# Two Strassen pairs of the recurrence's projections placed ahead of attention, and a planner that counts eight transfers under way

## The chip, the cores and the metric

One core of one Trainium2 chip runs the whole layer in one launch. The metric is the device time in microseconds of one execution; the figure for a kernel is the median of several runs. The engines are TensorE (PE, with its weight loads PEld), VectorE (DVE), ScalarE (ACT), GpSimd (POOL) and the queue of SyncE (SP), which issues nearly all transfers.

## The reference

One layer over 1024 frames of width 1024, float32. The parts that matter here:

```python
proj = x @ w_in
q_a, k_a, v_a, f_a, q_b, f_b, i_b, g_b, gate_a, gate_b = jnp.split(proj, IN_SPLITS, axis=-1)
y_a = fox_attention(q_a, k_a, v_a, log_sigmoid(f_a + b_f))      # 8 heads of 64, causal softmax
# the recurrence: 4 heads of 128
f  = lbh + (1.0 - lbh) * jax.nn.sigmoid(f_b)                    # forget gates
qh = jax.nn.silu(q_b)                                           # queries
o_b = hgrn2_chunkwise(qh, 1.0 - f, i_b, jnp.log(f))
y_b = rms_norm(o_b) * norm_g * jax.nn.sigmoid(g_b)
merged = sigmoid(gate_a) * (y_a @ w_pa) + sigmoid(gate_b) * (y_b @ w_pb)
x = layer_norm(ALPHA * x + merged @ w_o, ...)
x = layer_norm(ALPHA * x + swiglu_ffn(x, w_ff_in, w_ff_out), ...)
```

## The kernel before

Each float32 product is made of three matmuls on a high and a low part (`mm3`: high by high, high by low, low by high). The parts come from `split`, which is one ACT cast and one DVE subtraction. A matmul of full size has a stationary tile of 128x128 and 512 moving columns.

The stages in order are: the values by Strassen's method (to about 85 us); queries and keys of attention, four pairs of heads by Strassen's method (`qk_strassen`, called by `qk_all` in the order of the table `QORDER`); attention, eight heads (`attention`); the recurrence, four heads (`hgrn`); the gates by Strassen's method; the merge and output projection; the first layer norm; the feed-forward block; the second layer norm. Strassen's method takes the two halves of the contraction and the two halves of the frames, and makes two output blocks with 7 products of 12 matmuls, 84 in all. The plain way takes 2 x 48 = 96.

The recurrence needs three projections for each of its heads: the forget gate (index 1 of `w_b`), the query (index 0) and the output gate (index 2). `hgrn_project` makes each the plain way: `weights` loads and splits 512 KB, `project` runs 24 matmuls for each half of the frames into a bank named `bps`, ACT applies the sigmoid, and DVE multiplies for the query. That is 12 projections and 576 matmuls. They depend on nothing in attention, so they stand between attention's own matmuls and between those of the recurrence, as do parts of the gates (`gate_part`, banks named `ge`).

No engine's order is written by hand. Every call is recorded by `Plan`, and `schedule` places the calls on the engines one by one by modelled costs (`cost`), latencies (`LAT`), free buffers (each tile has a tag, and each tag a number of buffers) and due times found by `latest`. `improve` repeats that 36 times and keeps the best plan. So a change in one place reorders the whole program. For transfers the planner has one stream with a rate, a start latency, and a wait per issue on SP. `plan.behind` makes a call wait for another one.

Names that the steps use: `qk_d` is the DRAM buffer through which queries and keys pass; `q2_0`, `k2_0`, `kl_0` are the query, high key and low key of attention head 0 as loaded from it; `box1` holds the forget sums and the causal mask; `kb` is a tag with 4 buffers, `hl` one with 2. The keys `k2` and `kl` take `kb`. Two `kb` buffers also hold the operand of product p3 until the last pair of queries and keys is through. `wb` is a weight of the recurrence, `lp`, `dg`, `kdt`, `up`, `op`, `ot` are the recurrence's banks, and `hk`, `qf`, `at` its working tiles.

Of the kernel before, what the change touches and what calls it, by code (L numbers as in the profile page):

```python
# [16 lines left out]
P = 128  # L17
S = 1024
# [15 lines left out]
FIRST = 8  # L34
WARM = 7
ROUNDS = 36
QORDER = ((0, "hl", ("s", "pt", "s")), (1, "kb", ("h", "pv", "h")), (2, "hl", ("s", "pt", "s")), (3, "hl", ("h", "s", "h")))
MARGIN = 1.06
SLACK = 400.0
SWITCH = 300.0  # L40
# [23 lines left out]
class Plan:  # L64

    LAT = {"PE": 197.0, "ACT": 131.0, "DVE": 128.0, "POOL": 66.0, "SP": 2500.0}
    OWN = {"PE": 0.0, "ACT": 0.0, "DVE": 127.0, "POOL": 60.0, "SP": 2500.0}
    SOFT, LANDS, RATE = 950.0, 1050.0, 190.0  # L70
    SETS = {AF.Exp: 0, AF.Ln: 0, AF.Sigmoid: 1, AF.Silu: 2}

# [69 lines left out]
    def cost(self, eng, method, outs, ins, kw):  # L142
        o = outs[0]
        n = o.free_size()
        psum = any(str(a.space).endswith("PSUM") for a in ins)
        if eng == "PE":
            dt = ins[0].dtype
            if method == "transpose":
                return 109.0
            if dt == F32:  # L150
                return 2 * max(112.0, n / 1.2 + 2)
            return n / 2.4 + 13.4 if n > 128 else 111.0
        if eng == "ACT":
            d = n / 1.2 + (52 if psum else 94) + 95 * (o.partition_size() == DH)
            if "accum_out" in kw:
                d += 93
            return d + 93 * sum(isinstance(kw.get(x), bass.AP) for x in ("scale", "bias"))
        if eng == "DVE":
            scal = sum(1 for a in ins if a.free_size() == 1 and n > 1)
            two = method in ("tensor_scalar", "tensor_copy") and not psum  # L160
            if method == "reciprocal":
                return 90.0
            if method == "tensor_tensor_scan":
                return n * 2.1 + 69
            if method == "copy_predicated":
# [12 lines left out]
        return float(o.nbytes()) / 300.0  # L178

    def kind(self, call):  # L180
        return next((self.SETS.get(x) for x in call[2] if isinstance(x, AF)), None)
# [1 line left out]
    def schedule(self, slack, wait):  # L183
# [12 lines left out]
        free = {q: 600.0 for q in self.queues}  # L196
        dma_free = 0.0
        ring = [0.0] * RING
        fifo, slots = {}, {}
        for name, i in sorted(self.first.items(), key=lambda kv: (self.turn[kv[1]], kv[1])):  # L200
            tag, bufs = self.tiles[name][:2]
# [13 lines left out]
        while done < len(calls):  # L215
            best = None
            for q, av in avail.items():
                for i in av:
                    t = max(free[q], ready[i])
                    ok = True  # L220
                    need = {}
                    for name in calls[i][6]:
                        if name in held:
                            continue
                        tag = self.tiles[name][0]
                        k = need.get(tag, 0)
                        if tag not in LOOSE and name not in self.loose and (len(fifo[tag]) <= k or fifo[tag][-1 - k] != name):
                            ok = False
                            break
                        if len(slots[tag]) <= k:  # L230
                            ok = False
                            break
                        t = max(t, sorted(slots[tag])[k][0] + 60)
                        need[tag] = k + 1
                    if not ok:
                        continue
                    if self.lands[i]:
                        t = max(t, ring[-RING])
                    if q == "ACT":
                        kind = self.kind(calls[i])  # L240
                        if kind is not None and kind != table:
                            t += wait
                    if best is None or (t, self.rank[i]) < best[:2]:
                        best = (t, self.rank[i], i, q)
# [9 lines left out]
            if q == "SP":  # L254
                start = max(t + 100, dma_free)
                dma_free = start + d
                free[q] = t + 500
                fin = dma_free
            else:
                if q == "ACT":  # L260
                    kind = self.kind(c)
                    if kind is not None and kind != table:
                        table = kind
                        t -= wait
                        d += 1283
# [125 lines left out]
def trunk(ctx: ExitStack, tc, a: dict, out: bass.AP):  # L391
# [341 lines left out]
    def qk_strassen(p, wtags, btags, last=False):  # L733

        g, u = (take(t, [KC, P], f"w{n}{p}_r") for t, n in zip(wtags, "qk"))
        for b, t in enumerate((g, u)):
            sync.dma_start(t, a["w_qk"][b, p])
        b11, b12, b21, b22 = g[:, :4], u[:, :4], g[:, 4:], u[:, 4:]
        p1, p5 = (half("ph", f"qk{p}_{i}") for i in ("p1", "p5"))
        oa, ob, oc = (bank(t, f"qk{p}_{t}") for t in btags)  # L740

        def mul(n, src, o, first):
            lane = lanes[0]
            lanes[0] ^= 1
            T = [take(f"w{x}{lane}", [4, P], f"Tqk{p}{n}{x}", F32R) for x in "hl"]
# [5 lines left out]
        def put(b, hf, o):  # L751
            hi, lo = (half("gt" if n else "tt", f"qk{p}_{b}{hf}{n}", F32R) for n in range(2))
# [8 lines left out]
        mul("p1", b11, oa, True)  # L761
        act.copy(p1, oa)
        dve.tensor_sub(b12, b12, b11)
        mul("p5", b12, oc, True)
        if last:
            for c in range(4):
                raw = half("tt", f"a21_{c}")
                sync.dma_start(raw, a["xT"][c][:, hs(1)])
                split(A21[0][c], A21[1][c], raw)
        t2 = take("tt", [4, P], f"wqk{p}_t2")  # L770
        dve.tensor_sub(t2, b22, b12)
        mul("p2", b21, ob, True)
        dve.tensor_add(p1, ob, p1)
        put(0, 0, p1)
        mul("p6", t2, oa, False)
        u2 = half("tt", f"qk{p}_u2")
        act.copy(u2, oa)
        dve.tensor_sub(b11, t2, b11)
        mul("p7", b11, oa, False)
        act.copy(p5, oa)  # L780
        dve.tensor_add(p5, oc, p5)
        put(1, 1, p5)
        mul("p3", b22, oc, False)
        dve.tensor_add(u2, oc, u2)
        put(1, 0, u2)
        dve.tensor_sub(b21, b21, t2)
        mul("p4", b21, oa, False)
        put(0, 1, oa)

    def qk_load(h):  # L790
        p, i = divmod(h, 2)
# [5 lines left out]
        return q2, k2, kl  # L797

    def qk_all():
        for p, w, b in QORDER:  # L800
            qk_strassen(p, (w, w), b, p == QORDER[-1][0])

    scored = []

    def attention(p):
        for i in range(2):
            h = 2 * p + i
            plan.behind = tuple(scored[:h - 1][-1:]) if h >= 2 else ()
            q2, k2, kl = qk_load(h)
            plan.behind = ()  # L810

# [73 lines left out]
    dve.memset(raw, 1.0)  # L885
    act.copy(ones, raw)
    lmask = const("lmask", [P, 2, MASKS], U16, "mask")
    sync.dma_start(ng, a["ng"])
    sync.dma_start(lbl, a["lbl"])
    lbe, lbs, lb, olb = (lbt[:, i, :] for i in range(4))  # L890
    dve.memset(mhalf, -0.5)
    dve.tensor_sub(lbe, lbl, lbl)
    act.activation(lbe, lbe, AF.Exp)
    dve.reciprocal(lbs, lbe)
    dve.tensor_mul(lbs, lbs, lbe)
    dve.tensor_sub(lb, lbs, lbs)
    dve.tensor_scalar(olb, lb, -1.0, 1.0, op0=ALU.mult, op1=ALU.add)

    yb_d = dram.tile([4, P, S], F32, name="yb_d")

# [4 lines left out]
    def hgrn_project(h):  # L905
        q, fk, sg = (full("qk", f"hb{n}{h}") for n in "qfg")
        for bi, dst in ((1, fk), (0, q), (2, sg)):
            plan.early = AHEAD
            w = weights(a["w_b"][bi, h], [KC, P], f"wb{bi}_{h}", 0)
            plan.early = 0  # L910
# [33 lines left out]
    def hgrn(h, qfg, box):  # L944
        q, fk, sg = qfg
        k = full("kb", f"hk{h}")
        act.activation(fk, fk, AF.Identity, scale=olb[:, h:h + 1], bias=lb[:, h:h + 1])
        pool.tensor_scalar(k, fk, -1.0, 1.0, op0=ALU.mult, op1=ALU.add)

        at = full("pf", f"at{h}")  # L950
# [1028 lines left out]
```

## Time and profile before

| what | us |
|---|---|
| median of 3 runs | 1420.11 |
| lowest and highest run | 1420.03 and 1420.58 |
| the profiled execution, device time | 1421.71 |
| its span, first to last instruction | 1420.0 |
| PE busy in the span | 1404.2 |
| DVE busy in the span | 1134.4 |
| ACT busy in the span | 649.2 |
| mean granted TensorE clock | 0.997 |

The profiled execution lies 1.60 us above the median of the runs, and 1.71 us of its time lie outside its span. A matmul's duration in the trace overlaps with the next one's, so the time that a matmul costs is read from the distance between two starts, or from a stretch's length over its count, and not from its mean duration.

### The profile page before, as it was taken

To read this page: it belongs to the slowest core of one execution; us is meant where nothing else is said; L and a number is where in the kernel's file an instruction comes from. 1 tells how busy PE (TensorE), PEld (TensorE's weight loads), DVE (VectorE), ACT (ScalarE), POOL (GpSimd) and SP (SyncE) were. 2 spreads that over 40 slices of the span, in tenths; PEclk is the share of its full clock that TensorE was granted. 3 is DMA by queue.
4 is the path that set the end of the run, shared out by engine and by line. 5 is a ranking of instruction groups with operands and counts; after the bars stand their busy time and mean duration, and the time that the engine had idled before them with its cause. 6 is when DMAs were issued, how large, how long until landed. Compare 5 with 4: busy or idle time off the path is not lost.

```text
span 1420.0 us, 19016 instructions
## 1 busy us (share of the span) xinstructions
PE 1404.2 (99%) x6650; PEld 1163.8 (82%) x6650; DVE 1134.4 (80%) x1986; ACT 649.2 (46%) x1175; POOL 87.3 (6%) x104
## 2 busy tenths in 40 slices
PE   9999989999999999999999999999999999999997
PEld 7788878888888888888887788888888888888886
DVE  7985868898776769678899879876687976789597
ACT  5534578874334433266438942233323334434330
POOL 0000134330000000000001000000000000000001
PEclk9999999999999999999999999999999999999999
DMA  7458999811113487446633536533334336878632
GB/s 270 155 171 265 298 267 279 242 67 45 32 56 136 144 246 214 154 156 230 237 131 119 198 125 203 197 119 98 104 111 137 115 107 203 313 260 274 217 125 89
DMA packets 99359, 245.16 MB, mean 173 GB/s; under 512 B 11440, under 2 KB 12592, under 8 KB 99264
## 3 DMA queue, kind: packets, MB, share of 16 engines
q1 hardware_dynamic: 98112, 239.76, 50.7%
q0 software_dynamic: 1152, 4.19, 1.6%
q8 instruction: 52, 0.85, 0.2%
q14 instruction: 43, 0.35, 0.1%
HBM read 181.20 MB, written 62.72 MB: 172 GB/s over the span
## 4 chain that ended last, share of the span: by engine, by line
PE 96%; DMA 2%; DVE 1%; ACT 1%; issue 0%; SPq 0%; POOL 0%; DVEq 0%; ACTq 0%; POOLq 0%
PE p L387 15%; PE fb L387 12%; PE bps L387 9%; PE gs L387 8%; PE fc L387 8%; PE fa L387 5%; PE vx L387 4%; PE oa L387 3%; PE pps L387 3%; PE fe L387 3%; PE qk_s L387 3%; PE qk_h L387 2%; PE ob L387 2%; PE vy L387 2%; PE pv L387 2%; PE pt L387 2%
## 5 line engine op out<-in xcount | busy, mean ns | idle before, releaser
L387 PE MATMUL p<-dp 128*128 128x512 f32 (+1 forms) x957 | 210.0, 382 | 0.0
L387 PEld LDWEIGHTS p<-dp 128*128 128x128 f32 x957 | 175.3, 188 | 34.8
L387 PE MATMUL fc<-xs,Tp 128*128 128x512 f32 x528 | 129.3, 389 | 0.0
L387 PE MATMUL fb<-xs,Tp 128*128 128x512 f32 x528 | 127.8, 389 | 0.0
L387 PEld LDWEIGHTS fc<-xs,Tp 128*128 128x128 f32 x528 | 99.0, 188 | 20.8 <-ACT Tp L387 0.3
L387 PEld LDWEIGHTS fb<-xs,Tp 128*128 128x128 f32 x528 | 99.1, 188 | 20.6
L387 ACT CAST Tp<-t 128x512 fp32r<-128x512 f32 x88 | 54.4, 621 | 127.9 <-PE fb L387 69.1
L387 DVE TENSOR_TENSOR Tp<-t,Tp 128x512 fp32r<-128x512 f32 x88 | 60.3, 689 | 32.9 <-ACT Tp L387 32.5
L387 PE MATMUL fa<-x,Tp 128*128 128x512 f32 x336 | 81.4, 389 | 0.0
L387 PE MATMUL bps<-xh,wb_h 128*128 128x512 f32 x192 | 77.1, 402 | 0.0
L387 PE MATMUL bps<-xl,wb_h 128*128 128x512 f32 x192 | 77.1, 401 | 0.0
L387 PE MATMUL bps<-xh,wb_l 128*128 128x512 f32 x192 | 76.9, 401 | 0.0
L387 PEld LDWEIGHTS fa<-x,Tp 128*128 128x128 f32 x336 | 63.1, 188 | 13.1
L387 ACT CAST dp<-dap 128x1024 fp32r<-128x1024 f32 (+1 forms) x42 | 41.2, 980 | 65.5 <-PE p L387 37.1
L387 POOL TENSOR_TENSOR norm<-norm,few 128x1 f32<-128x1 f32 x16 | 14.7, 919 | 905.5 <-DVE norm L387 905.5
L387 DVE TENSOR_TENSOR dp<-dap,dp 128x1024 fp32r<-128x1024 f32 (+1 forms) x42 | 47.6, 1133 | 25.1 <-ACT dp L387 24.9
L387 DVE TENSOR_TENSOR tl<-pt,th 128x512 fp32r<-128x512 f32 (+1 forms) x96 | 52.5, 553 | 14.4 <-ACT th L387 11.5
L387 PE MATMUL fb<-x,Tp 128*128 128x512 f32 x240 | 57.8, 389 | 0.0
L387 ACT CAST th<-pt 128x512 fp32r<-128x512 f32 (+1 forms) x96 | 45.8, 478 | 25.1 <-PE pt L387 18.4
L387 PEld LDWEIGHTS fb<-x,Tp 128*128 128x128 f32 x240 | 45.0, 188 | 9.4
L387 DVE TENSOR_TENSOR u<-fb,p 128x512 f32<-128x512 f32 x40 | 27.6, 690 | 22.5 <-PE fb L387 22.2
L387 POOL TENSOR_SCALAR p<-p,sums 128x128 f32<-128x128 f32 (+7 forms) x48 | 34.5, 730 | 127.3 <-PE qk_h L387 65.8
(996 smaller groups left out, 3498.1 us busy)
## 6 DMA issues: line engine op xcount, KB each, us to landing
dbp<-in_w_fo SPq DMA_DIRECT2D x45, 512.0 KB, 4.6
dap<-a_d SPq DMA_DIRECT2D x35, 512.0 KB, 4.7
wg_r<-in_w_ff SPq DMA_DIRECT2D x22, 512.0 KB, 4.0
wu_r<-in_w_ff SPq DMA_DIRECT2D x22, 512.0 KB, 3.8
a_d<-ar SPq DMA_DIRECT2D x42, 256.0 KB, 3.0
wop_r<-in_w_o SPq DMA_DIRECT2D x18, 512.0 KB, 3.5
a_d<-as SPq DMA_DIRECT2D x33, 256.0 KB, 3.2
qk_d<-qk SPq DMA_DIRECT2D x32, 256.0 KB, 4.5
```

Source lines behind the costliest of these rows:

```text
L387: getattr(q.engine, method)(*args, **kw)
```

## The change

The forget gates and queries of the recurrence's heads 2 and 3 are made as two Strassen pairs, each pair one forget gate and one query, ahead of the four pairs of attention. `QORDER` lists six pairs now. `qk_strassen` becomes `strassen_pair`, which `qk_pair` and the new `b_pair` call with what each does to its results. `b_pair` applies the sigmoid, the multiplication or the lower bound at once, writes the result to DRAM (`b_d`), and `hgrn_project` loads it instead of projecting. The small preparation of the lower bounds moves to the front. The planner's model of transfers changes: rates by kind of transfer, a latency of 2400 in place of 2500, 480 in place of 500 for an issue, and an issue waits until the eighth last transfer has landed. The loads of attention's heads 0 and 1 wait for product p2 of the last pair.

```diff
-QORDER = ((0, "hl", ("s", "pt", "s")), (1, "kb", ("h", "pv", "h")), (2, "hl", ("s", "pt", "s")), (3, "hl", ("h", "s", "h")))
+QORDER = ((((1, 2), (0, 2)), "hl"), (((1, 3), (0, 3)), "kb"), (0, "hl"), (1, "kb"), (2, "hl"), (3, "kb"))
+PAHEAD = tuple(b for p, _ in QORDER if not isinstance(p, int) for b in p)
...
-        return float(o.nbytes()) / 300.0
+        near = ins[0] if str(o.space).endswith("DRAM") else o
+        rate = 235.0 if near.partition_size() == DH else 220.0 if ins[0].ap[0][0] == 0 else 350.0
+        return float(o.nbytes()) / rate
...
+        under_way = [0.0] * 8
...
+                    if q == "SP":
+                        t = max(t, under_way[-8])
...
-                free[q] = t + 500
+                free[q] = t + 480
                 fin = dma_free
+                under_way.append(fin + self.LAT["SP"])
...
+    b_d = dram.tile([3, HB, P, S], F32, name="b_d")
+
+    def strassen_pair(name, srcs, wtags, btags, perm, put, last=False):
...
+        mul("p2", b21, ob, True)
+        scored[:] = [len(plan.calls) - 1]
...
+    def b_pair(which, wtags, btags):
+        name = "b" + "".join(f"{i}{h}" for i, h in which)
+        perm = which[0][0] < 2
+
+        def put(b, hf, o, sv):
+            bi, h = which[b]
+            if b == 0 and hf:
+                t = half("gt", f"{name}_o")
+                act.activation(sv(t), o, AF.Sigmoid)
+            elif bi == 0:
+                t = o
+                s = half("gt", f"{name}_s{hf}")
+                act.activation(s, t, AF.Sigmoid)
+                dve.tensor_mul(t, t, s)
+            else:
+                t = o
+                act.activation(t, t, AF.Sigmoid)
+            if bi == 1:
+                act.activation(t, t, AF.Identity, scale=olb[:, h:h + 1], bias=lb[:, h:h + 1])
+            if perm:
+                sync.dma_start(b_d[bi, h].rearrange("p (c h t) -> p h c t", c=2, h=2)[:, hf],
+                               t.rearrange("p (c t) -> p c t", c=2))
+            else:
+                sync.dma_start(b_d[bi, h, :, hs(hf)], t)
+
+        strassen_pair(name, [a["w_b"][bi, h] for bi, h in which], wtags, btags, perm, put)
...
-            plan.behind = tuple(scored[:h - 1][-1:]) if h >= 2 else ()
+            plan.behind = tuple(scored[:max(h, 1)][-1:])
...
         for bi, dst in ((1, fk), (0, q), (2, sg)):
+            if (bi, h) in PAHEAD:
+                sync.dma_start(dst, b_d[bi, h])
+                continue
...
-        act.activation(fk, fk, AF.Identity, scale=olb[:, h:h + 1], bias=lb[:, h:h + 1])
+        if (1, h) not in PAHEAD:
+            act.activation(fk, fk, AF.Identity, scale=olb[:, h:h + 1], bias=lb[:, h:h + 1])
```

Three places show how the order moves.

First, TensorE where attention begins. Banks `qk2` and `qk3` are the third and fourth pair of attention's queries and keys, `s0` the scores of head 0, `bps1_0` the forget gate of the recurrence's head 0. Before:

```order
L387 MATMUL qk2_s_262<-vs3l1_147,Tqk2p7h_277 128x512
L387 MATMUL qk2_s_262<-vs3h1_145,Tqk2p7l_278 128x512
L387 MATMUL qk2_pt_263<-xh1_67,Tqk2p2l_271 128x512
L387 MATMUL s0_0_0_331<-k2_0_325,q2_0_324 128x128
L387 MATMUL s0_0_0_331<-kl_0_326,q2_0_324 128x128
L387 MATMUL qk3_h_293<-xh0_66,Tqk3p1h_296 128x512
```

Now:

```order
L394 MATMUL qk3_h_348<-vs4h1_166,Tqk3p3h_369 128x512
L394 MATMUL qk3_h_346<-xl1_69,Tqk3p4h_373 128x512
L394 MATMUL s0_1_0_387<-k2_0_378,q2_0_377 128x256
L394 MATMUL qk3_h_346<-xh1_67,Tqk3p4l_374 128x512
L394 MATMUL qk3_h_348<-vs4l1_168,Tqk3p3h_369 128x512
...
L394 MATMUL s0_0_0_384<-k2_0_378,q2_0_377 128x128
L394 MATMUL s0_3_0_393<-k2_0_378,q2_0_377 128x512
L394 MATMUL qk3_h_346<-xl1_69,Tqk3p4h_373 128x512
```

The first scores stood ahead of nearly the whole last pair; they stand now among its last products, so most of that pair's matmuls no longer lie between the first scores and what follows from them.

Second, the queue of SP, where the operands of head 0 are loaded. `a21` are slices of the input, `wb1_0_r` and `we6_r` weights for the matmuls that run beside attention. Before:

```order
L387 DMA qk_d_189<-qk1_110_248 128x512
L387 DMA q2_0_324<-qk_d_189 64x1024
L387 DMA v_d_180<-v4_185 128x1024
L387 DMA k2_0_325<-qk_d_189 64x1024 x2
L387 DMA q2_0_324<-qk_d_189 64x1024
L387 DMA kl_0_326<-qk_d_189 64x1024 x2
L387 DMA qk_d_189<-qk1_111_249 128x512
L387 DMA wq3_r_289<-in_w_qk 128x1024
```

Now:

```order
L394 DMA qk_d_189<-qk2_011_341 128x512
L394 DMA q2_0_377<-qk_d_189 64x1024 x2
L394 DMA q2_1_451<-qk_d_189 64x1024
L394 DMA k2_0_378<-qk_d_189 64x1024 x2
L394 DMA wb1_0_r_960<-in_w_b 128x1024
L394 DMA q2_1_451<-qk_d_189 64x1024
L394 DMA a21_1_354<-in_xT 128x512
L394 DMA we6_r_1182<-in_w_g 128x1024
L394 DMA kl_0_379<-qk_d_189 64x1024 x2
L394 DMA qk_d_189<-qk3_000_360 128x512
```

The loads of head 0 stood between the writes of the second pair; they stand now behind the last write of the third pair, with other loads between `k2_0` and `kl_0`.

Third, TensorE in the recurrence's head 2, around the level of 16 frames (`lp2_16`). `bps1_3` is the forget gate of head 3, `ge` are parts of the gates, `ot1` the end of head 1. Before:

```order
L387 MATMUL lp2_8_1067<-qf2_1053,ke2_8_1066 128x128 x4
L387 MATMUL bps1_3_0_1096<-xl1_69,wb1_3_h1_1094 128x512
...
L387 MATMUL ot1_0_1020<-ident_164,ob1_0_1019 128x128 x4
L387 MATMUL ot1_1_1025<-ident_164,ob1_1_1024 128x128 x4
L387 MATMUL lp2_16_1069<-qf2_1053,ke2_16_1068 128x128 x4
L387 MATMUL bps1_3_1_1097<-xh0_66,wb1_3_h0_1092 128x512
```

Now:

```order
L394 MATMUL lp2_8_1106<-qf2_1092,ke2_8_1105 128x128 x4
L394 MATMUL ge4_1179<-xl1_69,we4_h1_1177 128x512
...
L394 MATMUL ge10_1203<-xl0_68,we10_h0_1199 128x512
L394 MATMUL lp2_16_1108<-qf2_1092,ke2_16_1107 128x128 x4
L394 MATMUL ge8_1195<-xh0_66,we8_h0_1191 128x512
...
L394 MATMUL ot1_1_1078<-ident_164,ob1_1_1077 128x128 x4
L394 MATMUL kdt2_0_1113<-ident_164,hk2_1090 128x128 x4
```

Where the projection of head 3 lay beside the recurrence, the parts of the gates lie now, and the last transposes of head 1 (`ot1_1`) have moved behind two more levels of head 2.

More of the change, by code (lines that the diff above doesn't have):

```diff
@@ L64 @@
 class Plan:
-    LAT = {"PE": 197.0, "ACT": 131.0, "DVE": 128.0, "POOL": 66.0, "SP": 2500.0}
-    OWN = {"PE": 0.0, "ACT": 0.0, "DVE": 127.0, "POOL": 60.0, "SP": 2500.0}
+    LAT = {"PE": 197.0, "ACT": 131.0, "DVE": 128.0, "POOL": 66.0, "SP": 2400.0}
+    OWN = {"PE": 0.0, "ACT": 0.0, "DVE": 127.0, "POOL": 60.0, "SP": 2400.0}
     SOFT, LANDS, RATE = 950.0, 1050.0, 190.0
@@ L731, in trunk, with pv, sv @@
     lanes = [0]
[L733 to L737, printed above, removed]
-        b11, b12, b21, b22 = g[:, :4], u[:, :4], g[:, 4:], u[:, 4:]
-        p1, p5 = (half("ph", f"qk{p}_{i}") for i in ("p1", "p5"))
-        oa, ob, oc = (bank(t, f"qk{p}_{t}") for t in btags)
+    scored = []
+    sync.dma_start(ng, a["ng"])
+    sync.dma_start(lbl, a["lbl"])
+    lbe, lbs, lb, olb = (lbt[:, i, :] for i in range(4))
+    dve.memset(mhalf, -0.5)
+    dve.tensor_sub(lbe, lbl, lbl)
+    act.activation(lbe, lbe, AF.Exp)
+    dve.reciprocal(lbs, lbe)
+    dve.tensor_mul(lbs, lbs, lbe)
+    dve.tensor_sub(lb, lbs, lbs)
+    dve.tensor_scalar(olb, lb, -1.0, 1.0, op0=ALU.mult, op1=ALU.add)
+    b_d = dram.tile([3, HB, P, S], F32, name="b_d")
+    def strassen_pair(name, srcs, wtags, btags, perm, put, last=False):
+        g, u = (take(t, [KC, P], f"w{n}{name}_r") for t, n in zip(wtags, "qk"))
+        for src, t in zip(srcs, (g, u)):
+            sync.dma_start(t, src)
+        b11, b12, b21, b22 = g[:, :4], u[:, :4], g[:, 4:], u[:, 4:]
+        p1, p5 = (half("ph", f"{name}_{i}") for i in ("p1", "p5"))
+        oa, ob, oc = (bank(t, f"{name}_{t}") for t in btags)
+        def pv(o):
+            return o.rearrange("p (j c t) -> p c j t", c=2, t=P) if perm else o
+        def sv(t):
+            return t.rearrange("p (c j t) -> p c j t", c=2, t=P) if perm else t
         def mul(n, src, o, first):
@@ L744, in mul @@
             lanes[0] ^= 1
-            T = [take(f"w{x}{lane}", [4, P], f"Tqk{p}{n}{x}", F32R) for x in "hl"]
+            T = [take(f"w{x}{lane}", [4, P], f"T{name}{n}{x}", F32R) for x in "hl"]
             split(*T, src)
@@ L749, in mul, with qk_pair @@
                 mm3(o, T[0][:, c], T[1][:, c], vops[n][0][c], vops[n][1][c], first and c == 0, c == 3, more)
-        def put(b, hf, o):
-            hi, lo = (half("gt" if n else "tt", f"qk{p}_{b}{hf}{n}", F32R) for n in range(2))
+        mul("p1", b11, oa, True)
+        act.copy(sv(p1), pv(oa))
+        dve.tensor_sub(b12, b12, b11)
+        mul("p5", b12, oc, True)
+        if last:
+            for c in range(4):
+                raw = half("tt", f"a21_{c}")
+                sync.dma_start(raw, a["xT"][c][:, hs(1)])
+                split(A21[0][c], A21[1][c], raw)
+        t2 = take("tt", [4, P], f"w{name}_t2")
+        dve.tensor_sub(t2, b22, b12)
+        mul("p2", b21, ob, True)
+        scored[:] = [len(plan.calls) - 1]
+        dve.tensor_add(sv(p1), pv(ob), sv(p1))
+        put(0, 0, p1, sv)
+        mul("p6", t2, oa, False)
+        u2 = half("tt", f"{name}_u2")
+        act.copy(sv(u2), pv(oa))
+        dve.tensor_sub(b11, t2, b11)
+        mul("p7", b11, oa, False)
+        act.copy(sv(p5), pv(oa))
+        dve.tensor_add(sv(p5), pv(oc), sv(p5))
+        put(1, 1, p5, sv)
+        mul("p3", b22, oc, False)
+        dve.tensor_add(sv(u2), pv(oc), sv(u2))
+        put(1, 0, u2, sv)
+        dve.tensor_sub(b21, b21, t2)
+        mul("p4", b21, oa, False)
+        put(0, 1, pv(oa), sv)
+    def qk_pair(p, wtags, btags, last):
+        name = f"qk{p}"
+        def put(b, hf, o, sv):
+            hi, lo = (half("gt" if n else "tt", f"{name}_{b}{hf}{n}", F32R) for n in range(2))
             if b == 0:
@@ L759, in put @@
                 sync.dma_start(qk_d[p, 2 * b + n, :, hs(hf)], f(t))
[L761 to L788, printed above, removed]
+        strassen_pair(name, [a["w_qk"][b, p] for b in range(2)], wtags, btags, False, put, last)
+    def b_pair(which, wtags, btags):
+        name = "b" + "".join(f"{i}{h}" for i, h in which)
+        perm = which[0][0] < 2
+        def put(b, hf, o, sv):
+            bi, h = which[b]
[18 more added lines that the diff above has]
+        strassen_pair(name, [a["w_b"][bi, h] for bi, h in which], wtags, btags, perm, put)
     def qk_load(h):
@@ L799, in qk_all @@
     def qk_all():
-        for p, w, b in QORDER:
-            qk_strassen(p, (w, w), b, p == QORDER[-1][0])
-    scored = []
+        BT = (("s", "pt", "s"), ("h", "pv", "h"))
+        for n, (p, w) in enumerate(QORDER):
+            last = n == len(QORDER) - 1
+            b = ("h", "s", "h") if last else BT[n % 2]
+            if isinstance(p, int):
+                qk_pair(p, (w, w), b, last)
+            else:
+                b_pair(p, (w, w), b)
     def attention(p):
```

10 lines of the change are left out of this document (removed).

## The prediction

> **What bounds the kernel now.** I read the page's busy times first, then a table of stretches, then the waits of TensorE and the chain that ended last. The page:
>
> ```profile
> PE 1404.2 (99%) x6650; PEld 1163.8 (82%) x6650; DVE 1134.4 (80%) x1986; ACT 649.2 (46%) x1175; POOL 87.3 (6%) x104
> ```
>
> TensorE is busy 99% of a span of 1420.0 us. Since matmuls overlap in the trace, I check that by stretches (us; busy time and instructions of PE, PEld, DVE, ACT, POOL; granted clock; DMA share; GB/s). The rows are: queries and keys of attention, the start of attention, the rest of attention, the recurrence, gates to output projection, and the first layer norm:
>
> ```profile
> 85.00:164.00 79.00, 79.00 (x352) 65.18 (x351) 53.88 (x97) 37.26 (x69) 1.98 (x2) 1.00 0.76 249
> 164.00:206.00 42.00, 37.23 (x190) 30.44 (x190) 29.46 (x99) 29.91 (x64) 13.38 (x17) 0.96 0.94 277
> 206.00:320.00 114.00, 113.29 (x673) 97.28 (x672) 98.52 (x311) 96.77 (x208) 43.94 (x54) 1.00 0.70 200
> 320.00:500.00 180.00, 179.72 (x1010) 154.24 (x1009) 136.30 (x232) 77.05 (x179) 13.11 (x11) 1.00 0.25 85
> 500.00:740.00 240.00, 240.00 (x1060) 198.75 (x1059) 198.92 (x310) 100.58 (x165) 0.00 (x0) 1.00 0.61 197
> 740.00:820.00 80.00, 79.06 (x373) 62.30 (x372) 71.09 (x130) 67.48 (x132) 6.91 (x8) 1.00 0.47 157
> ```
>
> Between 500 and 740 us 1060 full-size matmuls take 240.00 us, 226.4 ns each, with no idle time. That is what a matmul costs here. TensorE loses 4.77 us at the start of attention (42.00 less 37.23), 0.71 in the rest and 0.28 in the recurrence. So almost every matmul taken out should shorten the span, as long as the other engines keep up. The waits of TensorE say what the loss was:
>
> ```profile
> PE pv L387 <- ACT th L387: 3.4, 1, 3.4
> PE s L387 <- DVE soft L387: 1.4, 1, 1.4
> ```
>
> The chain that ended last (start, length) names transfers in the same stretch:
>
> ```profile
> 168.67 7.67 DMA kl<-qk_d
> 176.90 8.70 DMA qk_d<-qk
> 193.63 9.83 DMA box<-nf_d
> ```
>
> So the start of attention waits, through DVE and ACT, for data that SP brings late while the DMA engines are 94% busy.
>
> **The matmuls.** The plain projections are three groups, 576 matmuls:
>
> ```profile
> L387 PE MATMUL bps<-xh,wb_h 128*128 128x512 f32 x192 | 77.1, 402 | 0.0
> L387 PE MATMUL bps<-xl,wb_h 128*128 128x512 f32 x192 | 77.1, 401 | 0.0
> L387 PE MATMUL bps<-xh,wb_l 128*128 128x512 f32 x192 | 76.9, 401 | 0.0
> ```
>
> Four of the 12 projections go: 4 x 48 = 192 matmuls, 192 x 0.2264 = 43.5 us of TensorE that lay inside attention and the recurrence. Two pairs come: 2 x 84 = 168 matmuls, 38.0 us, ahead of attention. The net is 24 matmuls, 24 x 0.2264 = 5.4 us, on the path wherever TensorE is full. The Trainium skill (Perfetto Trace Analysis, section Identifying the Most-Contended Engine) says that matmul busy time is a poor measure and that the LDWEIGHTS share should be read instead. By that, TensorE has 18% to spare (82% on the page), and the sum for this term could be 0. The trace disagrees: in the packed stretch 500 to 740 us the share is 198.75 of 240.00, 83%, at a pitch that the matmuls set. Here 83% is full.
>
> **DVE and ACT.** Rows (count, busy us, mean ns):
>
> ```profile
> L387 DVE TENSOR_TENSOR wb_l<-wb_r,wb_h 128x512 fp32r<-128x512 f32 x24 | 17.8, 743 | 13.2 <-ACT wb_h L387 13.0
> L387 DVE TENSOR_TENSOR hbq<-bps,hbq 128x512 f32<-128x512 f32 x8 | 5.5, 688 | 3.7 <-ACT hbq L387 3.7
> L387 DVE TENSOR_TENSOR wk_r<-wk_r,wq_r 128x512 f32<-128x512 f32 x4 | 2.8, 689 | 1.0 <-DMA wk_r<-in_w_qk 1.0
> L387 ACT CAST wb_h<-wb_r 128x512 fp32r<-128x512 f32 x24 | 14.9, 620 | 24.7 <-PE bps L387 22.7 <-issue 1.9
> L387 ACT ACTIVATE hbf<-hbf,few 128x1024 f32<-128x1024 f32 x4 | 5.0, 1249 | 0.1
> L387 ACT ACTIVATE hbf<-bps 128x512 f32<-128x512 f32 x8 | 4.8, 597 | 0.5 <-PE bps L387 0.3
> ```
>
> Removed from attention and recurrence: on DVE 8 splits x 0.743 + 4 products x 0.688 = 8.7 us; on ACT 8 casts x 0.620 + 8 sigmoids x 0.597 + 2 lower bounds x 1.249 = 12.2 us. Added ahead of attention, for each pair on DVE: 7 splits, 4 differences of weights, 3 sums, 2 query products, 16 x 0.69 = 11.0 us in 19.0 us of matmuls (58%). The queries and keys, at 53.88 of 79.00 (68%), already run without loss, so this costs nothing; ACT there is at 47% and is no nearer a limit. If that cover went, each pair would still need less DVE time than PE time.
>
> The other side is what is left behind. From 164 to 500 us lie 336 us, DVE busy 29.46 + 98.52 + 136.30 = 264.3 us, 79%. After the change TensorE needs 336 - 43.5 = 292.5 us there, and DVE still 264.3 - 8.7 = 255.6, which is 87%. What DVE can do beside attention is seen in single slices:
>
> ```profile
> 220.00:240.00 20.00, 20.00 (x120) 17.14 (x119) 15.43 (x53) 18.20 (x40) 7.24 (x10) 1.00 1.03 317
> 240.00:260.00 20.00, 20.00 (x119) 17.35 (x118) 16.69 (x55) 17.69 (x41) 8.06 (x10) 1.00 0.92 247
> 280.00:300.00 20.00, 19.29 (x114) 16.20 (x114) 17.80 (x54) 15.91 (x36) 8.18 (x11) 1.00 0.27 80
> 300.00:320.00 20.00, 20.00 (x115) 16.94 (x114) 18.76 (x44) 16.00 (x31) 6.14 (x5) 1.00 0.18 65
> ```
>
> In 280 to 320 us it was busy 36.56 of 40 us (91%) while TensorE lost 0.71. ACT reached 18.20 of 20 at 220 us without a loss on TensorE. So 87% can be held for a while; whether for 290 us, no row shows. The bounds: no cost if it holds; at that row's 1.8% of loss, 292.5 x 0.018 = 5.2 us in place of the 1.0 lost now, so +4.2; and far more if it does not hold (last rival). I take +1.5, nearer the lower end: 180 of the present 336 us run at a loss of 0.28 us, and the slices at 220 and 240 us lose nothing.
>
> **The transfers and the start of attention.** Median times to landing (us):
>
> ```profile
> qk_d<-qk SPq DMA_DIRECT2D x32, 256.0 KB, 4.5
> wb_r<-in_w_b SPq DMA_DIRECT2D x12, 512.0 KB, 3.6
> q<-qk_d SPq DMA_DIRECT2D x16, 256.0 KB, 4.3
> k<-qk_d SPq DMA_DIRECT2D x16, 256.0 KB, 6.5
> kl<-qk_d SPq DMA_DIRECT2D x16, 256.0 KB, 7.0
> ```
>
> Ahead of attention come 4 weights of 512 KB, which move forward, and 8 writes of 256 KB: 4.2 MB in 38 us. At the 249 GB/s of the first stretch 38 us carry 9.5 MB, so the backlog that now runs into attention shrinks by some 5 MB, or 21 us of transfer. Attention itself loses up to 2.1 MB of weights. The 4 loads of `b_d` (512 KB, 2.1 MB) fall into the recurrence, where the DMA engines are 25% busy. Their 4 issues on SP, and the 8 of the writes, cost nothing there.
>
> Against that, the loads of head 0 are issued later relative to their use. Before, the last was issued 11 us ahead of the first score (SP's issue, then TensorE):
>
> ```profile
> 130.28 1.23 SPq L387 DMA_DIRECT2D kl<-qk_d  x2
> ...
> 141.23 0.22 PE L387 MATMUL s<-k,q 128*128 128x128 f32 x1
> ```
>
> Now the keys need the two `kb` buffers of the last pair's weights, which are free when that pair's last weight is split, and the first score stands a few matmuls before the pair's end. Behind `k2_0` on SP wait two weight loads, a slice of the input and `kl_0`; behind `s0` on TensorE waits everything, since matmuls run in order. The new wait on product p2 of the last pair comes before that point and decides less. The bounds: the whole present loss goes, 4.77 us of idle time and 4% of clock over 42 us (1.7 us), so -6.4; or a full landing of `kl`, 7.0 us, comes on top, +7.0. I take -1.0: less backlog and transfers costed closer to their true times on one side, a later start on the other.
>
> The rest of the program is planned anew, too. The first layer norm loses 0.94 us of 80; I take no change, within +-2.
>
> **Sum.** -5.4 (matmuls) + 1.5 (DVE) - 1.0 (start of attention) = -4.9 us. The profiled execution took 1421.71 us, 1.71 outside its span of 1420.0, so it would take 1416.8. The median of the three runs, 1420.11, lies 1.60 lower than that execution; so I forecast **1415.2 us**. This kernel's runs lie within 0.55 us of each other, and 0.2% is 2.8 us: under 1417.3 is faster, over 1422.9 slower.
>
> **Rivals.**
> - *The start of attention becomes free.* With 5 MB less backlog the waits of 3.4 and 1.4 us and the clock's dip go: 1420.1 - 5.4 - 6.4 = 1408.3. For it: all three waits come back to transfers in a stretch that is 94% busy. Against it: the later loads of head 0. 14%.
> - *The gain is taken back (no change).* The stretch from attention's start to the gates loses 1.8% as in 280 to 320 us: -5.4 + 4.2 = -1.2, about 1419, with the present loss at the start. For it: DVE at 87% on average leaves little room for its chain with TensorE. The skill's reading of the LDWEIGHTS share (page and section above) would end here as well, with 1420, as TensorE would not be the limit. The trace bears that out only where other engines hold it up. 20%.
> - *Slower.* In the recurrence and attention DVE's instructions wait on TensorE and ACT at each step, and DVE may not pass the 83% of the busiest slice at 220 to 260 us (16.69 of 20). Then the stretch takes 255.6 / 0.835 = 306 us in place of 292.5, +13.6, and the sum is 1420.1 - 5.4 + 13.6 = 1428. It decides from a DVE share under 255.6 / (292.5 + 8.2) = 85%. For it: the fillers that lay between the levels of a head are fewer, and two heads now run at once. Against it: 91% held for 40 us, and the slices at 220 to 260 had TensorE full, so they show no limit of DVE. 17%.
> - That the change does not do what it says is excluded: the order has 168 matmuls of the new pairs and 384 of the old projections.
>
> **Numbers.** The forecast has 49% (1410 to 1417.3); with the first rival the faster side has 63%, no change 20%, slower 17%. From 1407 to 1425 leaves out about 4% below and, as some of the slower cases end near their bound of 1422.9, about 13% above.
>
> **What would show it.** The `bps` groups fall from 192 to 128 each. The first score moves from 141 us to about 200: 38 us for the new pairs, and some 20 us of the last pair that now lie ahead of it. The recurrence ends, and the gates take TensorE alone, about 5 us earlier than before. DVE's share between attention's start and that point rises from 79% to about 87%. The waits on `th` and `soft` are under 5 us together. I am wrong if TensorE waits for `lp`, `dg` or `op` inputs from DVE for more than 4 us in the recurrence, if the first score waits for `k2` or `kl` over 3 us, or if the layer norm's loss changes by over 2 us.

## The result and the profile after

The changed kernel takes 1412.39 us, the median of 4 runs (1411.47 to 1412.99), against 1420.34 for the kernel before on the same chip (4 runs, 1420.03 to 1420.76). The ratio is 0.9941 with a 95% interval of 0.9927 to 0.9956: 8 us, or 0.6%, faster. The profiled executions took 1411.47 (after) and 1421.71 (before), so their spans differ by 10.3 us. That is 2.3 more than the medians do, because the one of before lies 1.4 above its median and the one of after 0.9 below. Two runs of the experiments below, one of 1580.49 us and one of 2208.61 us, had a mean granted clock of 0.834 and 0.598 and are left out of medians and ratios.

The page of the changed kernel (span; busy times):

```profile
span 1409.7 us, 19063 instructions
PE 1397.0 (99%) x6626; PEld 1158.7 (82%) x6626; DVE 1138.0 (81%) x2006; ACT 660.7 (47%) x1193; POOL 88.3 (6%) x104
```

TensorE is busy 7.2 us less (24 matmuls fewer, and less stretched by a low clock), and idle 12.7 us in place of 15.8. The same six stretches as in the prediction (us; PE, PEld, DVE, ACT, POOL busy and instructions; granted clock, DMA share, GB/s) show where:

```profile
85.00:164.00 79.00, 79.00 (x350) 65.21 (x349) 48.62 (x83) 38.67 (x67) 1.98 (x2) 1.00 0.56 177
164.00:206.00 42.00, 41.19 (x180) 33.13 (x179) 26.17 (x42) 18.29 (x33) 0.00 (x0) 1.00 0.79 250
206.00:320.00 114.00, 113.27 (x666) 96.81 (x667) 95.36 (x336) 103.42 (x222) 46.66 (x61) 1.00 0.94 266
320.00:500.00 180.00, 180.00 (x1057) 156.43 (x1057) 157.39 (x303) 94.84 (x223) 22.92 (x22) 1.00 0.37 121
500.00:740.00 240.00, 239.69 (x1061) 198.05 (x1060) 203.05 (x322) 104.01 (x168) 1.11 (x2) 1.00 0.59 189
740.00:820.00 80.00, 78.50 (x368) 62.13 (x367) 68.97 (x121) 65.05 (x129) 5.86 (x6) 1.00 0.50 168
```

Row by row against before: the idle time from 164 to 206 us falls from 4.77 to 0.81, and the clock there rises from 0.96 to 1.00. From 206 to 500 us the idle time is 0.73 (0.99 before), although DVE is busier. The gates lose 0.31 (0.00), the layer norm 1.50 (0.94). Attention now begins at the end of the second row, so the row to look at beside it is the third: it loses 0.73 us with the DMA engines 94% busy. Waits of TensorE:

```profile
PE vy L394 <- DVE idle L394: 1.2, 1, 1.2
PE x1t L394 <- ACT r L394: 0.9, 1, 0.9
PE oa L394 <- ACT Top4h L394: 0.6, 1, 0.6
PE s L394 <- DVE soft L394: 0.6, 1, 0.6
PE bps L394 <- DVE qk_u L394: 0.5, 1, 0.5
```

The wait of `pv` on `th` (3.4 us) is gone, that of `s` on `soft` is 0.6 in place of 1.4. The longest that is left (`vy`) is at the program's start. The transfers did not become quick. Median landing times:

```profile
qk_d<-qk SPq DMA_DIRECT2D x32, 256.0 KB, 3.9
q<-qk_d SPq DMA_DIRECT2D x16, 256.0 KB, 5.0
k<-qk_d SPq DMA_DIRECT2D x16, 256.0 KB, 5.2
wb_r<-in_w_b SPq DMA_DIRECT2D x8, 512.0 KB, 6.4
kl<-qk_d SPq DMA_DIRECT2D x16, 256.0 KB, 6.7
```

`q` and `wb_r` land later than before (4.3 and 3.6) and `kl` about as late; only the writes to `qk_d` and the loads of `k` (5.2, from 6.5) land sooner. What changed is mainly that TensorE does not run into them.

**A dip in the clock that belongs to the wait.** In the profile of before, stretches of 2 us around the wait on `th`:

```profile
182.00:184.00 2.00, 0.64 (x3) 0.19 (x1) 0.00 (x0) 0.00 (x0) 0.00 (x0) 1.00 1.01 339
184.00:186.00 2.00, 0.01 (x1) 0.01 (x1) 0.03 (x1) 0.31 (x2) 0.00 (x0) 1.00 1.03 405
186.00:188.00 2.00, 2.00 (x8) 1.86 (x9) 0.27 (x2) 1.99 (x4) 0.00 (x0) 0.51 1.09 407
188.00:190.00 2.00, 2.00 (x9) 1.69 (x9) 0.86 (x4) 1.31 (x4) 1.39 (x3) 0.64 0.85 187
190.00:192.00 2.00, 2.00 (x13) 1.74 (x13) 2.00 (x7) 2.00 (x5) 0.00 (x0) 1.00 0.19 68
```

After 3.35 us of idleness the clock is at half for about 3.4 us, which costs 1.7 us more than the wait itself ((1 - 0.51) x 2 + (1 - 0.64) x 2). The Trainium skill (TensorE: Matmul & The Clock Gate, Part 1) says that the clock falls to half after an idle window of about 3.4 us and returns after a busy one, and that the windows run freely. The half clock and its length agree in this execution; on the threshold two of the runs below do not.

### The profile page after: what moved, and what is told of

Read it like the earlier page. It is cut to its first block, busy times and chain, and to the rows that moved or that the text cites. A ratio compares the mean times of both kernels' runs of the same rounds, so it can differ in the third digit from the quotient of the medians.

```text
span 1409.7 us, 19063 instructions
## 1 busy us (share of the span) xinstructions
PE 1397.0 (99%) x6626; PEld 1158.7 (82%) x6626; DVE 1138.0 (81%) x2006; ACT 660.7 (47%) x1193; POOL 88.3 (6%) x104
## 4 chain that ended last, share of the span: by engine, by line
PE 96%; DMA 1%; DVE 1%; SPq 0%; ACT 0%; issue 0%; DVEq 0%
PE p L394 15%; PE fb L394 12%; PE fc L394 8%; PE gs L394 8%; PE bps L394 6%; PE fa L394 5%; PE vx L394 4%; PE fe L394 3%; PE pps L394 3%; PE oa L394 3%; PE vy L394 3%; PE pv L394 2%; PE s L394 2%; PE qk_s L394 2%; PE ge L394 2%; PE ob L394 2%
## 5 line engine op out<-in xcount | busy, mean ns | idle before, releaser
L394 PE MATMUL bps<-xl,wb_h 128*128 128x512 f32 x128 | 52.0, 406 | 0.0
L394 PE MATMUL bps<-xh,wb_h 128*128 128x512 f32 x128 | 51.4, 402 | 0.5 <-DVE qk_u L394 0.5
L394 PE MATMUL bps<-xh,wb_l 128*128 128x512 f32 x128 | 51.5, 402 | 0.0
```

What stands on the lines that cost most here:

```text
L394: getattr(q.engine, method)(*args, **kw)
```

## The experiments

All times are medians; the ratio is to the kernel before, run beside them. The kernel before itself measured 1420.68, 1421.15 and 1421.53 us in the three groups of runs (16, 27 and 11 runs), each on another chip, so kernels of different groups are best compared by their ratios.

**The planner's model of transfers alone.** Theory P: the time comes from the planner, which times transfers better. Theory M: it comes from the matmuls taken out. The kernel before with the new model and nothing else:

```diff
...
-        return float(o.nbytes()) / 300.0
+        near = ins[0] if str(o.space).endswith("DRAM") else o
+        rate = 235.0 if near.partition_size() == DH else 220.0 if ins[0].ap[0][0] == 0 else 350.0
+        return float(o.nbytes()) / rate
...
+                    if q == "SP":
+                        t = max(t, under_way[-8])
...
```

> The kernel before with the planner's new model of transfers (rates by kind, eight under way, 2400 and 480) and nothing else: no Strassen pairs of the recurrence, no new wait of heads 0 and 1. Theory M (the matmuls give 5.4 us, and the start of attention got cheaper because the pairs ahead of it thin out the transfers): the new model alone moves nothing but the plan's luck, 1418 to 1422 us, and the waits of 3.4 and 1.4 us at the start of attention stay. Theory P (the new model removes the waits at the start of attention): 1415 to 1417 us, with TensorE idle under 2 us between 160 and 210 us (4.8 before).

Measured: 1416.06, ratio 0.9966 (0.9953 to 0.998). Its row for the start of attention:

```profile
164.00:206.00 42.00, 41.92 (x240) 35.26 (x241) 36.94 (x126) 35.71 (x77) 16.14 (x21) 1.00 0.99 287
```

The same stretch at a DMA share of 99% now loses 0.08 us and no clock, with no pair moved. So P holds for this part: a third of a per cent comes from the order alone, and the DMA engines need not be less busy for it.

**The pairs alone.** The changed kernel with the old model:

```diff
...
-        near = ins[0] if str(o.space).endswith("DRAM") else o
-        rate = 235.0 if near.partition_size() == DH else 220.0 if ins[0].ap[0][0] == 0 else 350.0
-        return float(o.nbytes()) / rate
+        return float(o.nbytes()) / 300.0
...
-                    if q == "SP":
-                        t = max(t, under_way[-8])
...
```

> The changed kernel with the planner's old model of transfers (one rate of 300, latency 2500, issue 500, no limit on transfers under way). Theory M: nearly all of the gain is kept, 1411.5 to 1414.5 us. Theory P: only the 24 matmuls are kept, 1414.5 to 1416 us, and TensorE idles 3 us or more at the start of attention.

Measured: 1415.02, ratio 0.9954 (0.9936 to 0.9972). So the pairs are worth 5.7 us by themselves, the model 4.6, both 8. They don't add up, since both take away the long wait at the start of attention: in this kernel the largest waits there are under 1 us as well. There are more of them, though: from 164 to 320 us TensorE is idle 3.61 us, against 1.54 in the changed kernel. The time lies in P's range and above M's, so M's "nearly all of the gain" did not hold.

**Another plan of the same program.** `improve` varies its plans by random numbers; another seed gives another order of the changed kernel and of the kernel before.

```diff
-        vary = np.random.default_rng(1)
+        vary = np.random.default_rng(2)
```

> The changed kernel with another seed of the random numbers by which the planner varies its 30 later rounds. Same work, another plan. It says how much of a difference of a few us is the luck of one plan. Both theories: within 2 us of the changed kernel, 1410.4 to 1414.4. If it lies 3 us or more away, differences of that size between any two plans here prove nothing.

> The kernel before with another seed of the planner's random numbers. Same work, another plan. Both theories: within 2 us of the kernel before, 1418.3 to 1422.3. If it comes out 3 us lower, the plan of before was an unlucky one and a part of the change's gain beyond the 5.4 us of matmuls is luck.

Measured: the changed kernel 1413.10 (0.9941, 0.9923 to 0.9959), as with its own seed. The kernel before 1419.12 (0.9993, 0.9976 to 1.0009), no difference that can be told. Its profiled execution again waits at the start of attention, on another operand:

```profile
PE bps L387 <- DVE qk L387: 4.4, 1, 4.4
```

That execution was the slowest of its ten runs (1426.15); the four at a mean clock of 0.999 average 1417.0. So the gain isn't one lucky plan, and of two plans by the old model both show a long wait there. The second plan of the changed kernel isn't free of waits either: its scores wait 2.4 us for DVE (`soft`), and the clock dips behind it:

```profile
PE s L394 <- DVE soft L394: 2.4, 1, 2.4
```

```profile
252.00:254.00 2.00, 0.76 (x3) 0.76 (x4) 1.11 (x5) 1.16 (x2) 0.00 (x0) 0.85 1.01 260
254.00:256.00 2.00, 2.00 (x6) 1.47 (x5) 0.66 (x2) 0.00 (x0) 0.00 (x0) 0.50 1.02 387
256.00:258.00 2.00, 2.00 (x11) 1.75 (x10) 1.33 (x5) 0.76 (x3) 0.00 (x0) 0.80 1.03 408
```

**One pair.** Only the pair of head 3:

```diff
-QORDER = ((((1, 2), (0, 2)), "hl"), (((1, 3), (0, 3)), "kb"), (0, "hl"), (1, "kb"), (2, "hl"), (3, "kb"))
+QORDER = ((((1, 3), (0, 3)), "hl"), (0, "kb"), (1, "hl"), (2, "kb"), (3, "hl"))
```

> The changed kernel with one pair (forget gate and query of head 3) ahead of attention; head 2 is projected the plain way again. 12 matmuls more than the changed kernel, 12 fewer than before. Theory 1 (each matmul out of the stream gives its pitch of 226 ns, the rest of the gain belongs to the planner's model): halfway between the planner alone (1416.1) and the changed kernel (1412.4 to 1413.1), 1414 to 1415.5 us. Theory 2 (the gain of the pairs is mostly the room they make for transfers ahead of attention): one pair of 19 us gives most of it, 1412 to 1413.5 us.

Measured: 1416.39, ratio 0.9964 (0.995 to 0.9978), outside the ranges of both theories. That is the new model's gain and nothing visible of the 12 matmuls (2.7 us). Its waits on `th` are 1.8 us in all and on `kl` 1.2, and from 164 to 320 us TensorE is idle 4.06 us, against 1.54 with two pairs. That is enough to hide 2.7 us, though the intervals don't settle it. The table also moves the last pair's weights from `kb` to `hl` here, and so do the three pairs below: these two kernels differ from the changed kernel in more than the number of pairs.

**Three pairs.** The output gates of heads 2 and 3 go ahead too:

```diff
-QORDER = ((((1, 2), (0, 2)), "hl"), (((1, 3), (0, 3)), "kb"), (0, "hl"), (1, "kb"), (2, "hl"), (3, "kb"))
+QORDER = ((((1, 2), (0, 2)), "hl"), (((1, 3), (0, 3)), "kb"), (((2, 2), (2, 3)), "hl"), (0, "kb"), (1, "hl"), (2, "kb"), (3, "hl"))
```

> The changed kernel with a third pair ahead of attention, the output gates of heads 2 and 3. 12 matmuls fewer than the changed kernel (2.7 us), and 96 fewer to lie beside attention and the recurrence, so that DVE's share from attention's start to the gates rises from 86% to about 92%. Theory 1 (TensorE stays the limit as DVE held 95% in single slices): 1409.5 to 1411.5 us. Rival (DVE becomes the limit there): TensorE idles 3 us or more in that stretch and the time is 1412.5 us or more.

Measured: 1419.84, ratio 0.9991 (0.9981 to 1.0001), although it has 12 matmuls fewer still. Attention, recurrence, and the largest waits:

```profile
206.00:320.00 114.00, 107.19 (x597) 90.10 (x597) 86.68 (x288) 86.11 (x189) 36.90 (x49) 0.99 1.01 274
320.00:500.00 180.00, 175.53 (x1058) 151.27 (x1057) 163.24 (x346) 100.73 (x242) 34.42 (x34) 1.00 0.39 129
```

```profile
PE pv L394 <- ACT th L394: 2.7, 1, 2.7
PE s L394 <- DVE soft L394: 2.5, 1, 2.5
PE pt L394 <- DVE tl L394: 2.2, 2, 1.5
```

TensorE is idle 11.28 us in these 294 us (6.81 + 4.47), against 0.73 with two pairs. DVE's share of the whole 294 us is no higher (249.9, 85%; with two pairs 252.8, 86%), but that is an average over two stages with different limits. In attention the three waits of 2.7, 1.5 and 2.5 us make nearly all of the 6.81, and behind each of them stands a transfer, with the DMA engines fully busy:

```profile
ACT qk L394 <- DMA qk_d<-qk: 3.7, 1, 3.7
DVE tl L394 <- DMA qk_d<-qk: 3.1, 1, 3.1
DVE p L394 <- DMA box<-nf_d: 2.4, 1, 2.4
```

ACT and DVE work in the order of the plan: while ACT stands at an instruction that waits for a write to `qk_d`, `th` behind it is not made. In the recurrence the loss falls where DVE is nearly full. From 380 to 500 us, with three pairs and then with two:

```profile
380.00:500.00 120.00, 116.23 (x712) 101.10 (x712) 114.43 (x204) 56.63 (x146) 14.11 (x11) 1.00 0.40 138
```

```profile
380.00:500.00 120.00, 120.00 (x710) 105.06 (x709) 105.99 (x191) 57.09 (x147) 11.16 (x10) 1.00 0.45 146
```

DVE is busy 95% there in place of 88%, TensorE loses 3.77 us, and 2.6 us of that are waits for DVE. So the expected rival, DVE as the limit, holds for the end of the recurrence, while attention lost its time to transfers. How much of either is due to the 96 matmuls that no longer lie there, and how much to the plan and its buffers, no run separates. The clock dips here too, after the wait of 2.7 us:

```profile
228.00:230.00 2.00, 0.69 (x3) 0.20 (x2) 0.80 (x2) 1.45 (x4) 0.00 (x0) 1.00 1.07 259
230.00:232.00 2.00, 0.57 (x1) 0.34 (x2) 1.77 (x7) 2.00 (x5) 0.00 (x0) 0.78 1.03 324
232.00:234.00 2.00, 2.00 (x7) 1.63 (x7) 2.00 (x8) 2.00 (x5) 0.17 (x1) 0.50 1.03 213
```

That is less idle time than the window of 3.4 us that the Trainium skill names (page and section above).

**The saved matmuls put back.** The changed kernel with 24 extra matmuls of 128x512, a second time product p1 of attention's first two pairs (those two products count double):

```diff
+            if name in ("qk0", "qk1") and n == "p1":
+                for c in range(4):
+                    mm3(o, T[0][:, c], T[1][:, c], vops[n][0][c], vops[n][1][c], first and c == 0, c == 3, more)
```

> The changed kernel with 24 matmuls added again ahead of attention: the product p1 of attention's first two pairs is accumulated twice into its bank (so queries and keys of those pairs are not the reference's). No transfer, no DVE and no ACT work is added. Theory 1 (a matmul costs its pitch): 24 x 0.2264 = 5.4 us over the changed kernel, 1417.3 to 1418.8 us. Theory 2 (the gain of the pairs is room for transfers, not matmuls): the same room or more, under 1415 us.

Measured: 1416.34, ratio 0.9965 (0.9952 to 0.9977), so 3.4 us over the changed kernel by the ratios and 3.95 by the medians. That is below the 5.4 of theory 1 (1417.3 to 1418.8) and above theory 2: the matmuls do cost time. The interval of the difference of the two ratios is estimated from theirs at 0.7 to 6.1 us, and holds 5.4. The page:

```profile
PE 1404.1 (99%) x6650; PEld 1164.1 (82%) x6650; DVE 1137.6 (80%) x2006; ACT 661.2 (47%) x1193; POOL 86.0 (6%) x104
```

The share of PEld stays at 82% while the time moves, which is what the prediction held against reading it as 18% to spare.

**The pairs placed later**, between attention's second and third pair of heads:

```diff
-QORDER = ((((1, 2), (0, 2)), "hl"), (((1, 3), (0, 3)), "kb"), (0, "hl"), (1, "kb"), (2, "hl"), (3, "kb"))
+QORDER = ((0, "hl"), (1, "kb"), (((1, 2), (0, 2)), "hl"), (((1, 3), (0, 3)), "kb"), (2, "hl"), (3, "kb"))
```

> The changed kernel with the two pairs of the recurrence third and fourth, behind attention's first two pairs. Same work and same number of matmuls. The queries and keys of heads 0 to 3 are in DRAM some 38 us sooner. If the start of attention still loses time because its operands are written late, TensorE's loss between 195 and 215 us (2.6 us in the changed kernel) goes and the time is 1410 to 1411.5 us; if it is set by the buffers of the last pair, it stays at 1411.5 to 1414 us.

Measured: 1413.93, ratio 0.9943 (0.9926 to 0.996), as the changed kernel. From 195 to 215 us TensorE loses 1.41 us, and in the changed kernel 1.54 (by its trace; the expectation has 2.6), so that loss stays. This other place ahead of attention makes no difference that can be told.

**The model in two parts.** Which part of the planner's model makes the order better: the limit of eight, or the truer rates (with the delays of 2400 and 480)? Each alone on the kernel before, and the changed kernel without the limit:

```diff
+        under_way = [0.0] * 8
...
+                    if q == "SP":
+                        t = max(t, under_way[-8])
...
+                under_way.append(fin + self.LAT["SP"])
```

> The kernel before with one part of the planner's new transfer model: no more than eight of SP's transfers are counted as under way; its rates and delays stay the old ones (300 bytes per ns). The whole model on this kernel gave a ratio of 0.9966 (some 4.7 us). Theory L (the limit of eight is what keeps the planner from sending more than the DMA engines carry at the start of attention): 1415.5 to 1417.5 us, and TensorE's loss between 164 and 206 us, 4.8 us before, falls to 2.5 or less. Theory R (the truer rates of the 64-partition and broadcast loads do it): no change, 1419.5 to 1421.5, with waits on th and soft together near 4.8 us as before. Theory Z (any new plan differs by about as much, as the other seed did with 1419.1): anywhere from 1417 to 1421, without a pattern in those waits.

```diff
...
-        return float(o.nbytes()) / 300.0
+        near = ins[0] if str(o.space).endswith("DRAM") else o
+        rate = 235.0 if near.partition_size() == DH else 220.0 if ins[0].ap[0][0] == 0 else 350.0
+        return float(o.nbytes()) / rate
...
-                free[q] = t + 500
+                free[q] = t + 480
```

> The kernel before with the other part of the planner's new transfer model: bytes per ns by the kind of transfer (235 for 64 partitions, 220 for a broadcast, 350 for the others in place of 300), 2400 ns to land in place of 2500, 480 ns between issues in place of 500; no limit on transfers under way. Theory R: 1415.5 to 1417.5 us, the loss between 164 and 206 us at 2.5 us or less. Theory L: no change, 1419.5 to 1421.5, waits on th and soft together near 4.8 us. Theory Z: anywhere from 1417 to 1421, without a pattern.

```diff
-        under_way = [0.0] * 8
...
-                    if q == "SP":
-                        t = max(t, under_way[-8])
...
-                under_way.append(fin + self.LAT["SP"])
```

> The changed kernel without the limit of eight transfers under way in the planner, with the new rates and delays. The changed kernel took 1412.4, with the old model altogether 1415.0. Theory L: 1414.3 to 1415.7, as with the old model, and waits at the start of attention as in that run. Theory R: 1411.5 to 1413.3, as the changed kernel. Theory Z: in between, 1412 to 1415.

Measured: the limit alone 1415.84 (0.9967, 0.9954 to 0.9979), the rates alone 1416.05 (0.9965, 0.9952 to 0.9979), the changed kernel without the limit 1416.64 (0.9966, 0.9955 to 0.9977). On the kernel before, each part brings what the whole model brings, so neither L nor R as stated holds: either one is enough to move the wait away. Both times lie below the range of theory Z (1417 to 1421). But all three plans with some new part are free of the long wait and both without are not, so which feature of the order does it, and whether any other disturbance of the model would, stays open. The start of attention with the limit alone, then with the rates alone:

```profile
164.00:206.00 42.00, 40.58 (x224) 34.21 (x223) 32.52 (x107) 34.26 (x70) 14.90 (x18) 1.00 1.03 295
```

```profile
164.00:206.00 42.00, 41.41 (x235) 35.00 (x234) 36.61 (x130) 34.62 (x79) 16.27 (x22) 1.00 1.01 294
```

With the pairs the limit does matter in these plans, by about 3.6 us by the ratios, and without it the rates are no better than the old model (1415.02). The 1416.64 lies above the ranges of all three theories. Of the kernel without the limit, the largest wait, at the first scores, and the stretches of 2 us behind it, from its slowest run (1420.31):

```profile
PE s L390 <- issue: 3.9, 1, 3.9
```

```profile
208.00:210.00 2.00, 1.08 (x4) 1.11 (x5) 0.00 (x0) 0.00 (x0) 0.00 (x0) 0.50 1.03 235
210.00:212.00 2.00, 2.00 (x7) 1.52 (x6) 0.25 (x1) 0.87 (x2) 0.00 (x0) 0.50 1.02 376
212.00:214.00 2.00, 2.00 (x6) 1.34 (x5) 1.96 (x4) 1.34 (x3) 0.00 (x0) 0.50 1.08 382
214.00:216.00 2.00, 2.00 (x10) 1.66 (x10) 1.46 (x8) 1.97 (x5) 0.00 (x0) 0.86 0.99 230
```

The chain of this kernel names what the scores waited for:

```profile
196.54 11.26 DMA k<-qk_d
```

The key was issued at 196.5 us (193.3 in the changed kernel), and landed after 11.3 us. This is the case that the prediction feared for the changed kernel (a full landing on top of the start), with `k` in the place of `kl`. The limit is not the only thing that keeps it away: the pairs with the old model have no limit either, issue the key at 196.3 us, and wait 0.9 us at most. Half clock for some 6 us follows the wait, in part while TensorE is still idle.

**Without the wait on product p2.**

```diff
-            plan.behind = tuple(scored[:max(h, 1)][-1:])
+            plan.behind = tuple(scored[:h][-1:]) if h >= 2 else ()
```

> The changed kernel without the new wait on product p2 of the last pair: the loads of heads 0 and 1 may be issued as soon as their buffers allow. In the order the first score then stands 12 rows of TensorE earlier. My prediction held that this wait decides little, since the buffers of the keys come free later than p2: same as the changed kernel within 1.5 us, 1411 to 1414, and the first score within 4 us of 202. Rival (the wait keeps early loads of the heads from delaying the pairs' own writes and reads in the transfer queue): 1415 to 1418 us, with waits for kl, k or soft of over 2 us at the start of attention.

Measured: 1410.91 (1409.27 to 1412.28), ratio 0.9929 (0.9917 to 0.9942), first score at 199.9 us. Its interval overlaps that of the changed kernel (0.9927 to 0.9956), so the wait on p2 costs nothing that could be told, and gains nothing: `kl` and `k` are waited for 0.9 and 0.7 us without it. Whether this version is 1.5 us faster stays open. Here `q` is loaded from 168.1 us on in place of 191.4, but the key is issued at 193.1 us, as before (193.3): as the prediction had it, something later than p2 decides when the keys are loaded.

## Why the prediction was right, and where its sum was not

The forecast was 1415.2 us with a range of 1407 to 1425, the measurement 1412.4. Direction held, and so did the matmuls' part of the mechanism. The two other terms were mis-sized, in the same direction, and the start of attention got cheap in another way than I gave. In the profiled executions the forecast (1416.8) misses by 5.3 us; that it misses by only 2.8 in the medians is luck: the two profiled executions lie on opposite sides of their medians.

- *Matmuls, -5.4.* The `bps` groups are as forecast:

```profile
L394 PE MATMUL bps<-xl,wb_h 128*128 128x512 f32 x128 | 52.0, 406 | 0.0
L394 PE MATMUL bps<-xh,wb_l 128*128 128x512 f32 x128 | 51.5, 402 | 0.0
L394 PE MATMUL bps<-xh,wb_h 128*128 128x512 f32 x128 | 51.4, 402 | 0.5 <-DVE qk_u L394 0.5
```

  Put back, the 24 matmuls cost 3.4 to 4.0 us, and the pairs alone gained 5.7, which holds a part of the start of attention too. 5.4 lies within both intervals, and the size of this term is known no better than that.
- *DVE left tight, +1.5.* Measured: nothing. From 206 to 500 us TensorE lost 0.73 us, less than before. From the first score to the gates, and in one 20 us slice of it:

```profile
202.00:475.00 273.00, 271.91 (x1604) 234.52 (x1603) 233.60 (x602) 185.72 (x408) 67.56 (x80) 1.00 0.59 172
...
320.00:340.00 20.00, 20.00 (x114) 16.76 (x114) 19.25 (x61) 16.79 (x38) 6.29 (x8) 1.00 0.26 80
```

  DVE's share there is 86% (233.60 of 273.00; forecast 87), and in the slice it is busy 96% while TensorE is full. So the lower bound was right, and the rival by which DVE may not pass 83% is wrong as to that number. The limit that it looked for came with the third pair, at 95% over 120 us.
- *Start of attention, -1.0.* Measured in the profiled executions: 3.96 us of idle time and 1.7 us of clock, together -5.6, near the lower bound of -6.4. The step that failed is the weighing of the later loads of head 0: I let them take back most of what the smaller backlog and the better model give, and the first score waits for neither `k2` nor `kl`. That cost exists, but of all plans with two pairs only the one with the new rates and no limit of eight pays it in full (a wait of 3.9 us). The other side of the weighing was not right either. The DMA engines are as busy where attention now begins (94%, 266 GB/s) as they were (94%, 277 GB/s), and the new model alone took the wait away at 99%. So the start got cheap by its order, and not because a backlog of 5 MB was gone. And I misread the wait of 3.4 us as one for data that comes late; ACT waited for a write to land:

```profile
ACT th L387 <- DMA qk_d<-qk: 3.7, 1, 3.7
```

  In the kernel `th` and the high parts of queries and keys take the same four buffers (`tt`), and such a part holds its buffer until its write to `qk_d` has landed.
- With the layer norm (+0.56) and the gates (+0.31) the parts of the profiled executions are -5.4 - 0.3 - 5.6 + 0.9 = -10.4, against a difference of the spans of -10.3. Against the medians (-8.0) that is about 2.3 too much; the start may differ between runs (below), which no trace shows.
- The first rival, a start that becomes free (1408.3), is nearly what the profiled execution shows, though not for its reason, the smaller backlog; the median lies between it and the forecast.
- Of the other signs, the first score came at 202.2 us (forecast about 200), and the waits on `th` and `soft` are 0.6 us. None of the signs of being wrong came: from 206 to 500 us TensorE waits for `soft` (0.6) and `qk_u` (0.5) and has no wait of note for `lp`, `dg` or `op`, and the layer norm's loss changed by 0.56 us. The merge, which follows the gates, starts at 598.4 in place of 609.9 us, a lead of 11.6, 6.6 more than the 5 forecast, of which the start gave 4.6 and the DVE term 1.8.

## What to carry to other kernels

Of three pairs taken out from beside attention and the recurrence, two paid together, and the third gave nearly all of it back, to late transfers in one stage and to a nearly full DVE in the next. DVE's average over both stages (85%) showed neither. So read TensorE's idle time and its waits stage by stage, follow each wait one engine further back, and only then look at the share of the engine that is found there. And price a wait of 3 us on TensorE at more than 3 us: the half clock behind it cost at least 1.3 to 2.7 us again here (estimates from the rows of 2 us in which TensorE was busy throughout, as in the 1.7 above).

## What the runs showed of the hardware that was not expected

The clock fell after idle times that differ. In the profiled executions of all kernels here, it fell in attention where TensorE had waited 2.4, 2.7, 3.4, 3.9 and 4.4 us, and in none with a longest wait of 2.2 or less. The changed kernel with another seed shows the shortest, 2.4 us, and half clock behind it.

The time of the kernel before may vary with that dip. In 27 of its runs, the mean granted clock and the time go together: 5 runs at 0.999 average 1417.8 us, 4 at 0.998 average 1421.3, 14 at 0.997 average 1421.6, and 4 at 0.996 average 1424.1. In the kernel with the matmuls put back they do not: 7 runs at 0.999 average 1416.6 us and 2 at 0.997 average 1416.5. That the dips differ from run to run is only fitted to the runs' clocks; a trace exists of one execution each.
